# Weight loads of the four FFNs in a trunk kernel: half of a pair's raw blocks in another pool, five chunks instead of four, two sums in place, X's differences by column

## Chip, cores and metric

The kernel runs on one core of a Trainium2 chip. The metric is the device time of one execution in microseconds (us). Before the change the median of three runs is 2451.7 us (2450.68 to 2454.08).

## What is computed

A trunk of DEPTH = 2 layers over 512 tokens of width 1024, all in float32. Each layer is a half-step FFN, a mixer (a bidirectional state-space scan in layer 0, neighbourhood attention in layer 1), a second half-step FFN, and a gated per-layer input embedding ("ple"). The change concerns the four FFNs; cut to that, the reference is:

```python
def swiglu(x, w_gu, w_down):
    g, u = jnp.split(x @ w_gu, 2, axis=-1)
    return (jax.nn.silu(g) * u) @ w_down

for i in range(DEPTH):
    h = h + 0.5 * swiglu(rmsnorm(h, ffn1_norm[i]), ffn1_w_gu[i], ffn1_w_down[i])
    h = h + mixer(rmsnorm(h, mix_norm[i]))
    h = h + 0.5 * swiglu(rmsnorm(h, ffn2_norm[i]), ffn2_w_gu[i], ffn2_w_down[i])
    gate = jax.nn.sigmoid(rmsnorm(h, ple_norm[i]) @ ple_w_gate[i])
    h = h + gate * rmsnorm(p[i] @ ple_w_proj[i], ple_post_norm[i])
```

The width between is 2816, or 22 columns of 128.

## The kernel before

**Products in three matmuls.** A float32 weight tile ("unit") is split into a hi part `wh` (a cast by ScalarE, L195) and a lo part `wl` (raw minus hi, by VectorE, called DVE, L197). The data are split in the same way, and each product is three matmuls: hi x hi, hi x lo, lo x hi. TensorE (PE) runs them; GpSimd (POOL) helps with a few products; SyncE (SP) issues the loads.

**The order of one FFN** (`ffn_order`, L49 to 66). First come six plain columns: for each, gate and up products against the normed data (L246, L249, L250), `activate` (L391 to 400), which makes the column's intermediate. The other 16 columns are made in pairs by a Strassen-like scheme of seven blocks, i = 0 to 6 (`block`, L446). A block is one unit of 128x1024 and 24 matmuls of 128x256 (L455 to 457). Between the blocks stand the "downs" of the chunk before: a down is one of the eight output tiles d, and it multiplies all intermediates of a chunk of columns by a unit of the down weights, three matmuls of 128x512 for each column; its result goes to h (L515). A chunk of six columns (three pairs, 21 blocks) thus carries eight downs of 18 matmuls between its blocks. After the last block stands `between` (in the second FFN of a layer, the ple's projection), then the eight downs of the last chunk, with which the next stage's norm begins.

**What the blocks work on.** The weights' side: for a pair the raws a11, a12, a21, a22 (1024 wide) and the sums s1 = a21 + a22 (L216), s2 = s1 - a11 (L217), s3 = a11 - a21 (L218), s5 = a12 - s2 (L223). Blocks 0 to 6 use a11, s2, s3, s1, a12, s5, a22. X's side: `sums(kk)` (L407 to 442) makes the differences of the normed data, for kk = 0 to 3, during the plain columns 2, 3 and 4, the last two together in column 4; each takes some twelve DVE operations (from L412 to L440). The norm's factor R is there from column 1 on, in the first FFN of all from column 2 on.

**After a block.** Its bank is added up by DVE (L461). At i = 5 and 6 a half of the pair's intermediate is finished: the add, for i = 5 a SiLU on ScalarE (L483), a product on GpSimd (L491), a cast on ScalarE (L496) and the lo part on DVE (L497). A down needs both parts of its columns.

**The loader** (L143 to 236). `plan` lists all units in the order in which TensorE uses them. `unit` keeps three split units ready. Raw tiles stand in `wr`, four buffers of 128x1024, `wh` and `wl` in three each. A plain or down unit ("u") brings on the next load and is split. At a pair's first block ("g") all four raws must be in `wr`, then s1, s2 and s3 are made in tiles of the shared pool `md` (24 buffers, also used for the intermediates and X's parts). Each block's split ("o") starts another load if fewer than three raws wait. A load is a DMA on SyncE's queue; it waits for the last reader of its buffer, and so do those behind it. The code fixes what is done; a scheduler decides where each engine's instructions stand.

Of the kernel before, what the change touches and what calls it, by code (L numbers as in the profile page):

```python
# [21 lines left out]
CHUNKS = ((0, 6), (6, 12), (12, 18), (18, 22))  # L22
# [47 lines left out]
def trunk(ctx, tc, A, out):  # L70
# [110 lines left out]
    loads = iter([src for what, a in todo if what != "o" for src in (a if what == "g" else [a])])  # L181
    todo = iter(todo)
    raws, ready, splits, blocks = [], [], [], {}

    def load_unit():
        src = next(loads, None)
        if src is not None:
            raw = wp.tile([P, 1024], F32, name=nm("wr"), tag="wr", bufs=4)
            n = src.shape[-1]
            sy.dma_start(out=raw[:, :n], in_=src)  # L190
            raws.append((raw, n))
# [11 lines left out]
    def prep_next():  # L203
        item = next(todo, None)
        if item is None:
            return False
        what, a = item
        if what == "u":
            load_unit()
            split_raw(*raws.pop(0))  # L210
        elif what == "g":
            while len(raws) < 4:
                load_unit()
            a21, a22, a11, a12 = [raws.pop(0)[0] for _ in range(4)]
            s1, s2, s3 = wide(), wide(), wide()
            v.tensor_add(out=s1, in0=a21, in1=a22)  # L216
# [1 line left out]
            v.tensor_sub(out=s3, in0=a11, in1=a21)  # L218
            blocks.update({0: a11, 1: s2, 2: s3, 3: s1, 4: a12, 6: a22})
        else:  # L220
            if a == 3:
                blocks[5] = wide()
                v.tensor_sub(out=blocks[5], in0=blocks[4], in1=s_of[0])  # L223
            if a == 1:
                s_of[0] = blocks[1]
            split_raw(blocks.pop(a), 1024)
            if len(raws) < 3:
                load_unit()
        return True

    s_of = [None]
# [122 lines left out]
    def ffn(norm, nxt, between=lambda: None, first=None):  # L354
# [144 lines left out]
        made = None  # L499
# [697 lines left out]
    begun = [(next(loads), wp.tile([P, 1024], F32, name=nm("wr"), tag="wr", bufs=4)) +  # L1197
# [168 lines left out]
```

## Time and profile before

| | before |
|---|---|
| median of 3 runs | 2451.7 us (2450.68 to 2454.08) |
| profiled execution | 2451.2 us, of which the span is 2449.2 us and 2.0 us lie outside it |
| mean granted clock of TensorE | 0.985 |
| busy: PE, DVE, ACT, POOL | 2367.2, 1771.3, 1105.3, 476.3 us |
| DMA | 265.93 MB, 109 GB/s in the mean |
| the four FFNs' first blocks start at | 74.20, 1006.21, 1446.15, 2071.31 us |
| their last eight downs start at | 360.22, 1293.74, 1732.07, 2359.06 us |

A row of the timeline gives the start in us, the duration in us, engine, line, operation, output and inputs, and in brackets the idle time of the engine just before it and what ended that. A matmul's duration overlaps the next one's; what counts is the distance of the starts. A row of the windows gives a stretch, its length, the busy time of each engine in it, the TensorE clock that was granted (1.00 is full), and the DMA engines' share. A row of waits gives the engine, the tile and line that waited, what it waited for, the total, the number and the longest.

### The profile page before, as it was taken

To read this page: it belongs to the slowest core of one execution; us is meant where nothing else is said; L and a number is where in the kernel's file an instruction comes from. 1 tells how busy PE (TensorE), PEld (TensorE's weight loads), DVE (VectorE), ACT (ScalarE), POOL (GpSimd) and SP (SyncE) were. 2 spreads that over 40 slices of the span, in tenths; PEclk is the share of its full clock that TensorE was granted. 3 is DMA by queue.
4 is the path that set the end of the run, shared out by engine and by line. 5 is a ranking of instruction groups with operands and counts; after the bars stand their busy time and mean duration, and the time that the engine had idled before them with its cause. 6 is when DMAs were issued, how large, how long until landed. Compare 5 with 4: busy or idle time off the path is not lost.

```text
span 2449.2 us, 34985 instructions
## 1 busy us (share of the span) xinstructions
PE 2367.2 (97%) x13810; PEld 2049.9 (84%) x13810; DVE 1771.3 (72%) x2437; ACT 1105.3 (45%) x1787; POOL 476.3 (19%) x373
## 2 busy tenths in 40 slices
PE   9999999999999999999999999999999999999898
PEld 8898888888888888898887889888877887899787
DVE  7877658877777767877656787775678758777657
ACT  5433335655566743433335443332437644333243
POOL 0110011345455621011103111110100011011120
PEclk9999999999999999999999999999999999999999
DMA  4233224544444542233223223232442322333222
GB/s 166 84 102 108 78 82 137 175 136 142 140 137 134 171 147 87 88 94 101 89 86 104 91 75 100 95 102 78 145 131 108 113 87 81 102 94 97 85 84 86
DMA packets 94341, 265.93 MB, mean 109 GB/s; under 512 B 11473, under 2 KB 12369, under 8 KB 94177
## 3 DMA queue, kind: packets, MB, share of 16 engines
q1 hardware_dynamic: 93888, 263.57, 34.0%
q8 instruction: 108, 1.77, 0.3%
q14 instruction: 57, 0.46, 0.1%
q10 hardware_dynamic: 288, 0.14, 0.0%
HBM read 253.40 MB, written 10.26 MB: 108 GB/s over the span
## 4 chain that ended last, share of the span: by engine, by line
PE 76%; DVE 12%; ACT 4%; POOL 4%; issue 2%; DMA 1%; SPq 0%; ACTq 0%; POOLq 0%; DVEq 0%
PE ps L250 17%; PE ps L246 17%; PE ps L249 16%; PE ps L455 7%; PE ps L457 7%; PE ps L456 7%; POOL t L491 2%; DVE wl L197 2%; ACT wh L195 2%; DVE md L218 2%; DVE md L216 1%; PE ps L833 1%; DVE md L217 1%; PE ps L811 1%; PE ps L854 1%
## 5 line engine op out<-in xcount | busy, mean ns | idle before, releaser
L246 PE MATMUL ps<-md,wh 128*128 128x512 f32 x2128 | 848.5, 399 | 36.2 <-ACT wh L195 31.9
L250 PE MATMUL ps<-md,wl 128*128 128x512 f32 x2128 | 838.9, 394 | 5.8 <-DVE wl L197 5.8
L249 PE MATMUL ps<-md,wh 128*128 128x512 f32 x2128 | 838.9, 394 | 0.2
L195 ACT CAST wh<-wr 128x1024 fp32r<-128x1024 f32 (+2 forms) x401 | 385.4, 963 | 648.1 <-PE ps L249 313.1
L197 DVE TENSOR_TENSOR wl<-wr,wh 128x1024 fp32r<-128x1024 f32 (+2 forms) x401 | 466.7, 1164 | 153.5 <-ACT wh L195 127.2
L246 PEld LDWEIGHTS ps<-md,wh 128*128 128x128 f32 x2128 | 405.3, 191 | 121.7 <-ACT wh L195 35.0
L250 PEld LDWEIGHTS ps<-md,wl 128*128 128x128 f32 x2128 | 405.2, 190 | 94.2 <-DVE wl L197 9.0
L249 PEld LDWEIGHTS ps<-md,wh 128*128 128x128 f32 x2128 | 406.5, 191 | 82.6 <-issue 3.3
L491 POOL TENSOR_TENSOR t<-t,t 128x512 f32<-128x512 f32 x64 | 121.7, 1902 | 978.4 <-ACT t L483 866.9
L457 PE MATMUL ps<-md,wl 128*128 128x256 f32 x1024 | 291.7, 285 | 4.4 <-DVE wl L197 4.4
L456 PE MATMUL ps<-md,wh 128*128 128x256 f32 x1024 | 291.1, 284 | 0.0
L455 PE MATMUL ps<-md,wh 128*128 128x256 f32 x1024 | 290.8, 284 | 0.0
L455 PE MATMUL ps<-sc,wh 128*128 128x256 f32 x768 | 222.6, 290 | 14.3 <-ACT wh L195 14.3
L457 PE MATMUL ps<-sc,wl 128*128 128x256 f32 x768 | 221.2, 288 | 12.6 <-DVE wl L197 12.6
L461 DVE TENSOR_TENSOR t<-ps,t 128x512 f32<-128x512 f32 x224 | 151.4, 688 | 108.3 <-PE ps L457 107.4
L456 PE MATMUL ps<-sc,wh 128*128 128x256 f32 x768 | 219.3, 286 | 0.0
L457 PEld LDWEIGHTS ps<-md,wl 128*128 128x128 f32 x1024 | 197.8, 193 | 5.2 <-DVE wl L197 5.2
L455 PEld LDWEIGHTS ps<-md,wh 128*128 128x128 f32 x1024 | 197.7, 193 | 1.9
L456 PEld LDWEIGHTS ps<-md,wh 128*128 128x128 f32 x1024 | 197.7, 193 | 1.9
L292 POOL TENSOR_TENSOR sq<-sq,sq 128x512 f32<-128x512 f32 x71 | 100.5, 1415 | 423.9 <-ACT sq L288 421.8
L195 ACT CAST wh<-md 128x1024 fp32r<-128x1024 f32 x128 | 131.7, 1047 | 109.1 <-PE ps L456 68.6
L515 DVE SCALAR_TENSOR_TENSOR hs<-ps,hs 128x512 f32<-128x512 f32 x128 | 88.1, 688 | 126.2 <-PE ps L250 126.2
(205 smaller groups left out, 2989.9 us busy)
## 6 DMA issues: line engine op xcount, KB each, us to landing
wr<-in_w_gw_dram SPq DMA_DIRECT2D x128, 512.0 KB, 3.4
wr<-in_w_dn_dram SPq DMA_DIRECT2D x96, 384.0 KB, 3.3
wr<-in_w_in_dram SPq DMA_DIRECT2D x65, 512.0 KB, 3.8
wr<-in_w_gu_dram SPq DMA_DIRECT2D x44, 512.0 KB, 3.4
hs<-crow SPq DMA_DIRECT2D x64, 256.0 KB, 4.0
wr<-in_w_qkv_dram SPq DMA_DIRECT2D x24, 512.0 KB, 3.5
wr<-in_w_dn_dram SPq DMA_DIRECT2D x32, 256.0 KB, 2.7
hs<-vrow SPq DMA_DIRECT2D x64, 128.0 KB, 3.5
```

Source lines behind the costliest of these rows:

```text
L195: splits.append(s.copy(out=hi[:, :n], in_=raw[:, :n]))
L197: v.tensor_sub(out=lo[:, :n], in0=raw[:, :n], in1=hi[:, :n])
L246: m = te.matmul(out=pt, lhsT=hi[:, sl], rhs=part(xp, 0, cols), start=first and k == 0, stop=False)
L249: te.matmul(out=pt, lhsT=hi[:, sl], rhs=part(xp, 1, cols), start=False, stop=False)
L250: te.matmul(out=pt, lhsT=lo[:, sl], rhs=part(xp, 0, cols), start=False, stop=last and k == n - 1)
L292: (v if fast else g).tensor_add(out=self.acc, in0=self.acc, in1=q)
L455: te.matmul(out=o, lhsT=hi[:, sl], rhs=xh, start=j == 0 and kk == 0, stop=False)
L456: te.matmul(out=o, lhsT=hi[:, sl], rhs=xl, start=False, stop=False)
L457: te.matmul(out=o, lhsT=lo[:, sl], rhs=xh, start=False, stop=j == 1 and kk == 3)
L461: v.tensor_add(out=k[to], in0=pt, in1=k[other])
L491: g.tensor_mul(out=x, in0=x, in1=gate)
L515: v.scalar_tensor_tensor(out=h[d], in0=pt, scalar=0.5, in1=h[d], op0=ALU.mult, op1=ALU.add)
```

## The change

It has four parts, all in the FFNs.

- **Raw blocks.** The pair's loads come in the order a21, a11, a22, a12. The first two go into `wr`, the other two into tiles of `md`. Loads run ahead by two counts, up to three waiting in `wr` and two in `md` (`top_up`, after each step of the plan), instead of one load per step.
- **Chunks** of 6, 4, 4, 4, 4 columns instead of 6, 6, 6, 4. The chunks of pairs are four of two pairs (14 blocks). An FFN has 40 downs instead of 32: 8 of 18 matmuls and 32 of 12, instead of 24 and 8. The number of matmuls is the same.
- **Two sums in place.** s3 is written over a21, and s5 over s2, right behind the split of block 1 instead of ahead of block 3.
- **X's differences by column.** One kk for each plain column from the first that has R: columns 1 to 4, and in the first FFN columns 2, 3, and then two in column 4 as before. The first pair of X11's parts lies in `sc` slots instead of `md`.

```diff
-CHUNKS = ((0, 6), (6, 12), (12, 18), (18, 22))
+CHUNKS = ((0, 6), (6, 10), (10, 14), (14, 18), (18, 22))
...
-                            yield "g", [gw[p - PLAIN // 2, x, y] for x, y in ((1, 0), (1, 1), (0, 0), (0, 1))]
+                            yield "g", [gw[p - PLAIN // 2, x, y] for x, y in ((1, 0), (0, 0), (1, 1), (0, 1))]
...
-    loads = iter([src for what, a in todo if what != "o" for src in (a if what == "g" else [a])])
+
+    loads = [x for what, a in todo if what != "o"
+             for x in (zip(a, ("wr", "wr", "md", "md")) if what == "g" else [(a, "wr")])]
...
+        src, tag = loads.pop(0)
+        raw = wp.tile([P, 1024], F32, name=nm("wr"), tag="wr", bufs=4) if tag == "wr" else wide()
...
+    def top_up():
+        while loads and waiting[loads[0][1]] < {"wr": 3, "md": 2}[loads[0][1]]:
+            load_unit()
...
-            while len(raws) < 4:
-                load_unit()
-            a21, a22, a11, a12 = [raws.pop(0)[0] for _ in range(4)]
-            s1, s2, s3 = wide(), wide(), wide()
+            a21, a11, a22, a12 = [take()[0] for _ in range(4)]
+            s1, s2 = wide(), wide()
             v.tensor_add(out=s1, in0=a21, in1=a22)
             v.tensor_sub(out=s2, in0=s1, in1=a11)
-            v.tensor_sub(out=s3, in0=a11, in1=a21)
-            blocks.update({0: a11, 1: s2, 2: s3, 3: s1, 4: a12, 6: a22})
+            v.tensor_sub(out=a21, in0=a11, in1=a21)
+            blocks.update({0: a11, 1: s2, 2: a21, 3: s1, 4: a12, 5: s2, 6: a22})
         else:
-            if a == 3:
-                blocks[5] = wide()
-                v.tensor_sub(out=blocks[5], in0=blocks[4], in1=s_of[0])
-            if a == 1:
-                s_of[0] = blocks[1]
-            split_raw(blocks.pop(a), 1024)
-            if len(raws) < 3:
-                load_unit()
+            split_raw(blocks[a], 1024)
+            if a == 1:
+                v.tensor_sub(out=blocks[5], in0=blocks[4], in1=blocks[5])
+        top_up()
...
-                if a[0] >= 2:
-                    for kk in ((0,), (1,), (2, 3), ())[a[0] - 2]:
-                        sums(kk)
+                while left and R[0] is not None:
+                    sums(left.pop(0))
+                    if a[0] < 4:
+                        break
```

In these rows of the order, names ending in a number are tiles: `wr` and `md` raws, `in_w_gw1_dram` the pairs' weights and `in_w_dn1_dram` the down weights of the first FFN. First SyncE's loads in the middle of the first FFN, before:

```order
L190 DMA wr282_1648<-in_w_dn1_dram 128x768
L190 DMA wr284_1679<-in_w_dn1_dram 128x768
L190 DMA wr291_1716<-in_w_gw1_dram 128x1024
L190 DMA wr298_1771<-in_w_gw1_dram 128x1024
L190 DMA wr313_1891<-in_w_gw1_dram 128x1024
L190 DMA wr319_1929<-in_w_gw1_dram 128x1024
L190 DMA wr325_1941<-in_w_dn1_dram 128x768
L190 DMA wr329_1976<-in_w_dn1_dram 128x768
```

and of the changed kernel:

```order
L192 DMA md269_1576<-in_w_gw1_dram 128x1024
L192 DMA md270_1578<-in_w_gw1_dram 128x1024
L192 DMA wr239_1377<-in_w_dn1_dram 128x512
L192 DMA wr245_1416<-in_w_dn1_dram 128x512
L192 DMA wr256_1492<-in_w_gw1_dram 128x1024
L192 DMA wr268_1574<-in_w_gw1_dram 128x1024
L192 DMA wr281_1661<-in_w_dn1_dram 128x512
L192 DMA wr287_1700<-in_w_dn1_dram 128x512
```

The two raws of `md` now stand ahead of down loads whose tiles were asked for earlier (the numbers 1377 and 1416 are lower than 1576), and only two pair loads in a row take `wr` buffers.

Next DVE at the change from one pair of columns to the next in the first FFN (in before inside its last chunk, after inside its second chunk). L497 (now L508) is the lo part of a half of the intermediate, L216 to L218 (now L227 to L229) are s1, s2, s3, L461 (now L472) is the add of block 6. Before:

```order
L497 TENSOR_TENSOR md_2536<-t_2444,md_2535 128x2x256
L216 TENSOR_TENSOR md_2543<-wr_2328,wr_2383 128x1024
L515 SCALAR_TENSOR_TENSOR hs_85<-ps_2540,hs_85 128x512
L217 TENSOR_TENSOR md_2544<-md_2543,wr_2472 128x1024
L218 TENSOR_TENSOR md_2545<-wr_2472,wr_2328 128x1024
L461 TENSOR_TENSOR t_2413<-ps_2574,t_2413 128x512
L223 TENSOR_TENSOR md_2702<-wr_2541,md_2544 128x1024
L497 TENSOR_TENSOR md_2536<-t_2413,md_2535 128x2x256
L197 TENSOR_TENSOR wl_2579<-wr_2553,wh_2577 128x768
```

and of the changed kernel:

```order
L508 TENSOR_TENSOR md_1690<-t_1604,md_1689 128x2x256
L227 TENSOR_TENSOR md_1695<-wr_1492,md_1576 128x1024
L472 TENSOR_TENSOR t_1549<-ps_1694,t_1549 128x512
L228 TENSOR_TENSOR md_1696<-md_1695,wr_1574 128x1024
L229 TENSOR_TENSOR wr_1492<-wr_1574,wr_1492 128x1024
L508 TENSOR_TENSOR md_1690<-t_1549,md_1689 128x2x256
L211 TENSOR_TENSOR wl_1739<-wr_1661,wh_1737 128x512
L527 SCALAR_TENSOR_TENSOR hs_81<-ps_1736,hs_81 128x512
L211 TENSOR_TENSOR wl_1759<-md_1696,wh_1757 128x1024
```

The down's split (`wl_2579` before, `wl_1739` now) stands behind the second half in both; s5 (L223) and an eviction (L515) have left the stretch ahead of it, and the add of block 6 now comes ahead of s2.

Last DVE where the plain columns end, in the second FFN. L412 is the first step of a kk of X's differences, L436 to L440 (now L447 to L451) its last ones, L393 and L396 (now L398 and L401) open the activation of column 5, L265 (now L270) is its lo part. Before:

```order
L436 TENSOR_TENSOR t_9205<-t_9193,t_9205 128x256
L412 SCALAR_TENSOR_TENSOR t_9215<-hs_8573,cst,rt_8881 128x512
L437 TENSOR_TENSOR t_9206<-t_9193,t_9205 128x256
L440 TENSOR_TENSOR sc_9202<-t_9205,sc_9201 128x512
L412 SCALAR_TENSOR_TENSOR t_9217<-hs_8749,cst,rt_8881 128x512
L440 TENSOR_TENSOR sc_9204<-t_9206,sc_9203 128x512
L419 TENSOR_TENSOR md_9195<-t_9215,md_9195 128x256
L265 TENSOR_TENSOR md_9221<-t_9217,md_9221 128x512
```

and of the changed kernel:

```order
L447 TENSOR_TENSOR t_9280<-t_9271,t_9280 128x256
L211 TENSOR_TENSOR wl_9303<-wr_9200,wh_9301 128x1024
L448 TENSOR_TENSOR t_9281<-t_9271,t_9280 128x256
L451 TENSOR_TENSOR md_9278<-t_9280,md_9278 128x512
L227 TENSOR_TENSOR md_9292<-wr_9135,md_9202 128x1024
L451 TENSOR_TENSOR md_9279<-t_9281,md_9279 128x512
L228 TENSOR_TENSOR md_9293<-md_9292,wr_9200 128x1024
L229 TENSOR_TENSOR wr_9135<-wr_9200,wr_9135 128x1024
```

Before, the last two kk follow each other in one plain column; now the last kk has that column alone, and the sums of the first pair (L227 to L229) follow it.

More of the change, by code (lines that the diff above doesn't have):

```diff
@@ L180, in trunk, with take @@
     todo = list(plan())
-    loads = iter([src for what, a in todo if what != "o" for src in (a if what == "g" else [a])])
+    loads = [x for what, a in todo if what != "o"
+             for x in (zip(a, ("wr", "wr", "md", "md")) if what == "g" else [(a, "wr")])]
     todo = iter(todo)
     raws, ready, splits, blocks = [], [], [], {}
+    waiting = {"wr": 0, "md": 0}
     def load_unit():
[L186 to L191, printed above, removed]
+        src, tag = loads.pop(0)
+        raw = wp.tile([P, 1024], F32, name=nm("wr"), tag="wr", bufs=4) if tag == "wr" else wide()
+        n = src.shape[-1]
+        sy.dma_start(out=raw[:, :n], in_=src)
+        raws.append((raw, n, tag))
+        waiting[tag] += 1
+    def take():
+        if not raws:
+            load_unit()
+        raw, n, tag = raws.pop(0)
+        waiting[tag] -= 1
+        return raw, n
+    def top_up():
+        while loads and waiting[loads[0][1]] < {"wr": 3, "md": 2}[loads[0][1]]:
+            load_unit()
     def split_raw(raw, n):
@@ L208, in prep_next @@
         if what == "u":
[L209 to L210 removed]
+            split_raw(*take())
         elif what == "g":
[L212 to L215 removed]
+            a21, a11, a22, a12 = [take()[0] for _ in range(4)]
+            s1, s2 = wide(), wide()
             v.tensor_add(out=s1, in0=a21, in1=a22)
             v.tensor_sub(out=s2, in0=s1, in1=a11)
[L218 to L223 removed]
+            v.tensor_sub(out=a21, in0=a11, in1=a21)
+            blocks.update({0: a11, 1: s2, 2: a21, 3: s1, 4: a12, 5: s2, 6: a22})
+        else:
+            split_raw(blocks[a], 1024)
             if a == 1:
[L225 to L228 removed]
+                v.tensor_sub(out=blocks[5], in0=blocks[4], in1=blocks[5])
+        top_up()
         return True
[L231 removed]
     def unit():
@@ L405, in ffn, with sc_r @@
         x11 = []
+        def sc_r():
+            return bp.tile([P, T], F32R, name=nm("sc"), tag="sc", bufs=15)
         def sums(kk):
@@ L413, in sums @@
                                        op1=ALU.mult)
-            if kk % 2 == 0:
-                x11.append(md(F32R))
+            if kk == 0:
+                x11[:] = [sc_r(), sc_r()]
+            elif kk == 2:
+                m = md(F32R)
+                x11[:] = m[:, 0, :], m[:, 1, :]
             c = slice(HT * (kk % 2), HT * (kk % 2) + HT)
-            hl = x11[-1][:, 0, c], x11[-1][:, 1, c]
+            hl = x11[0][:, c], x11[1][:, c]
             s.copy(out=hl[0], in_=x[0][:, lo_])
@@ L427, in room @@
                 if kk < 3:
-                    return [bp.tile([P, T], F32R, name=nm("sc"), tag="sc", bufs=15) for _ in range(2)]
+                    return sc_r(), sc_r()
                 m = md(F32R)
@@ L497, in halve @@
             v.tensor_sub(out=hl[1][:, :, c], in0=x, in1=hl[0][:, :, c])
-        made = None
+        made, left = None, [0, 1, 2, 3]
         for what, *a in ffn_order():
@@ L1195, in trunk @@
     n = Norm(C_G1)
-    begun = [(next(loads), wp.tile([P, 1024], F32, name=nm("wr"), tag="wr", bufs=4)) +
+    begun = [(loads.pop(0)[0], wp.tile([P, 1024], F32, name=nm("wr"), tag="wr", bufs=4)) +
              tuple(md(F32R).rearrange("p a b -> p (a b)") for _ in range(2)) for _ in range(4)]
@@ L1222, in trunk @@
             bring(*o)
-    for _ in range(3):
-        load_unit()
+    top_up()
     sy.dma_start(out=cst[:, C_GM:], in_=A["cst"][:, C_GM:])
```

## Prediction

> **What bounds the kernel now.** I read the page first, then TensorE's waits, then windows over the four FFNs, then single places on the timeline. TensorE works almost all of the time:
>
> ```profile
> span 2449.2 us, 34985 instructions
> PE 2367.2 (97%) x13810; PEld 2049.9 (84%) x13810; DVE 1771.3 (72%) x2437; ACT 1105.3 (45%) x1787; POOL 476.3 (19%) x373
> ```
>
> The change leaves the list of matmuls as it is, so only TensorE's stops can go, and what a stop does to its clock. Its waits (line, tile waited for, total us, times, longest) are nearly all for a weight unit's hi part (`wh`) or lo part (`wl`):
>
> ```profile
> PE ps L246 <- ACT wh L195: 31.9, 8, 4.4
> PE ps L457 <- DVE wl L197: 17.0, 20, 2.2
> PE ps L455 <- ACT wh L195: 14.3, 19, 2.1
> ...
> PE ps L246 <- ACT md L264: 3.8, 2, 1.9
> ```
>
> To see where they lie I cut each FFN in two. The start runs from the first block to the end of the fourth block and first down unit; the middle from there to the first of the last eight downs. The rows are starts, then middles, in the order of the FFNs (length; busy time of PE, PEld, DVE, ACT, POOL; granted clock; DMA share; GB/s):
>
> ```profile
> 74.20:98.16 23.96, 19.53 (x116) 17.96 (x115) 18.94 (x24) 8.62 (x11) 2.13 (x1) 0.86 0.23 72
> 1006.21:1028.70 22.49, 18.12 (x115) 16.44 (x114) 17.49 (x20) 8.61 (x11) 2.13 (x1) 0.92 0.26 77
> 1446.15:1469.23 23.08, 19.14 (x115) 17.50 (x114) 17.50 (x20) 8.71 (x11) 2.14 (x1) 0.85 0.24 74
> 2071.31:2093.83 22.52, 18.15 (x116) 16.51 (x115) 17.49 (x20) 8.62 (x11) 2.13 (x1) 0.92 0.24 76
> 98.16:360.22 262.06, 250.56 (x1665) 230.34 (x1664) 179.97 (x194) 93.27 (x114) 29.95 (x16) 0.98 0.30 92
> 1028.70:1293.74 265.04, 251.28 (x1665) 230.52 (x1663) 181.65 (x195) 94.99 (x116) 30.91 (x16) 0.98 0.31 95
> 1469.23:1732.07 262.84, 251.09 (x1664) 230.69 (x1663) 180.07 (x194) 93.28 (x114) 29.95 (x16) 0.98 0.30 91
> 2093.83:2359.06 265.23, 250.82 (x1665) 230.16 (x1663) 181.79 (x195) 94.98 (x116) 30.92 (x16) 0.98 0.31 95
> ```
>
> What they would last without stops comes from a stretch that has none; the rows are the first matmul of a block, of the next block, of a down unit, and of the block after it:
>
> ```profile
> 105.14 0.28 PE L455 MATMUL ps<-md,wh 128*128 128x256 f32 x1
> ...
> 108.02 0.28 PE L455 MATMUL ps<-sc,wh 128*128 128x256 f32 x1
> ...
> 110.89 0.40 PE L246 MATMUL ps<-md,wh 128*128 128x512 f32 x1
> ...
> 115.00 0.28 PE L455 MATMUL ps<-md,wh 128*128 128x256 f32 x1
> ```
>
> A block takes 108.02 - 105.14 = 2.88 us, a down of 18 matmuls 4.11 (0.228 each; one of 12 then 2.74). A start is 4 x 2.88 + 4.11 = 15.63, a middle 52 x 2.88 + 23 x 4.11 = 244.29. The starts sum to 92.05, 29.5 above nominal; the middles to 1055.17, 78.0 above. Two of the middles end in a wait of 1.9 for the ple's input (the L264 row), so the blocks' part is 78.0 - 3.8 = 74.2. These 29.5 and 74.2 are what the change can work on, and it can add to them.
>
> **The late loads go.** Before, DVE frees a raw buffer at the sums s1 to s3, and the next down's load waits for that. SyncE's queue, ScalarE and TensorE in one such place:
>
> ```profile
> 319.89 5.37 SPq L190 DMA_DIRECT2D wr<-in_w_dn_dram  x3
> ```
>
> ```profile
> 323.08 0.83 ACT L195 CAST wh<-wr 128x768 fp32r<-128x768 f32 x1 [2.64 <-DMA wr<-in_w_dn_dram]
> ```
>
> ```profile
> 323.97 0.80 PE L246 MATMUL ps<-md,wh 128*128 128x512 f32 x1 [4.15 <-ACT wh L195]
> ```
>
> ```profile
> 322.35:325.76 3.41, 1.79 (x5) 1.25 (x6) 1.81 (x2) 2.68 (x3) 0.00 (x0) 0.50 0.30 119
> 325.76:329.17 3.41, 3.41 (x10) 2.64 (x9) 1.50 (x2) 0.05 (x1) 0.00 (x0) 0.50 0.40 115
> ```
>
> It costs 4.15 us of idle and two windows at half clock, of which 0.9 and 1.7 us of work are lost: 6.75. After, the `md` pool takes half of a pair's raws and the SyncE order has every down's load a pair earlier, released by splits long done. A pair lasts 7 x 2.88 + 3 x 2.74 = 28.4 us, so I count no wait for a transfer. A raw for `md` that waited for its buffer would hold SyncE's queue, the next two downs' loads behind it; its buffer was last read a pair back, so I take 0, and 6.75 (rival E) as the other end.
>
> **The pair boundary, 28 times.** In chunks of two pairs each boundary runs block 5, block 6, down, block 0 of the next pair, down, block 1. Let T be the end of block 5, 108.02 in the stretch above, where DVE's and GpSimd's order was the one that it will be:
>
> ```profile
> 112.30 0.69 DVE L497 TENSOR_TENSOR md<-t,md 128x512 fp32r<-128x512 f32 x1 [1.83 <-ACT md L496]
> 112.91 1.22 DVE L216 TENSOR_TENSOR md<-wr,wr 128x1024 f32<-128x1024 f32 x1
> ...
> 115.78 2.32 DVE L218 TENSOR_TENSOR md<-wr,wr 128x1024 f32<-128x1024 f32 x1
> 118.02 0.68 DVE L497 TENSOR_TENSOR md<-t,md 128x512 fp32r<-128x512 f32 x1
> 118.65 1.23 DVE L197 TENSOR_TENSOR wl<-md,wh 128x1024 fp32r<-128x1024 f32 x1
> ```
>
> ```profile
> 109.89 1.73 POOL L491 TENSOR_TENSOR t<-t,t 128x512 f32<-128x512 f32 x1 [23.60 <-ACT t L483]
> 114.81 2.21 POOL L491 TENSOR_TENSOR t<-t,t 128x512 f32<-128x512 f32 x1 [3.19 <-DVE t L461]
> ```
>
> The product of block 5 (GpSimd) and its halves come first, then s1, the add, s2, then s3, which lasts 2.32 because GpSimd's second product runs beside it, then the second half, and only then the next split: T + 10.63. In the changed order that split is the `wl` of the down behind block 0. It is 512 wide; its price:
>
> ```profile
> L197 DVE TENSOR_TENSOR wl<-wr,wh 128x512 fp32r<-128x512 f32 x32 | 24.7, 773 | 20.1 <-ACT wh L195 20.1
> ```
>
> So it is there at T + 10.63 + 0.7 = T + 11.3. TensorE asks for it with that down's third matmul, at T + 2.88 + 2.74 + 2.88 + 2 x 0.228 = T + 8.96: a stop of 2.4. That holds for 5 boundaries in each FFN, 20 in all. Inside chunk 1 the downs still have 18 matmuls and 768 columns (between 0.77 and the 1.23 of 1024, say 1.0): asked for at 10.33, there at 11.6, 1.25 us, 4 times; from chunk 1 to 2 it is 11.3 against 10.33, 1.0 us, 4 times. Together 20 x 2.4 + 9.0 = 57 us.
>
> Each stop can also lower the clock. Neighbouring windows of the FFN2 start:
>
> ```profile
> 1008.42:1011.83 3.41, 1.81 (x16) 1.61 (x14) 3.41 (x4) 0.61 (x1) 0.00 (x0) 1.00 0.00 0
> 1011.83:1015.25 3.42, 1.72 (x12) 1.52 (x13) 3.42 (x5) 1.54 (x3) 0.53 (x1) 1.00 0.52 163
> 1015.25:1018.66 3.41, 3.41 (x16) 3.17 (x16) 1.58 (x3) 2.60 (x4) 1.60 (x1) 0.50 0.17 67
> ```
>
> TensorE busy for 1.72 of a window, and the next is granted 0.50; busy for 1.81, and the next is full. A half window costs 1.7 us of work. A stop of 2.4 leaves about 2.2 idle (the matmuls ahead drain meanwhile). The idle time needed is 3.41 - 1.72 = 1.69, and a window of 3.41 holds that much of 2.2 in (3.41 - 2.2) + 2 x (2.2 - 1.69) = 2.23 of 3.41 positions, 65%. So 13 of the 20 stops bring a half window: 22 us. The short ones bring none. The boundaries sum to 57 + 22 = 79 against 74.2: **+4.8**.
>
> The Trainium skill, "TensorE: Matmul & The Clock Gate", section "What's actually happening", puts the half clock behind an idle window of about 3.4 us; by it no stop of 2.4 would be followed by one, and the boundaries would be 57. The rows above disagree with it, since 1.72 busy of 3.42 was enough.
>
> **The sums of X by column.** In the last three FFNs one column of them per plain column fits under the matmuls, as it does before for the first ones (column's first and last entry on DVE; a plain column lasts 10.9, as the two L396 ends ahead of them show):
>
> ```profile
> 984.65 0.69 DVE L396 TENSOR_TENSOR t<-ps,rt 128x512 f32<-128x512 f32 x1 [0.65 <-PE ps L250]
> ...
> 994.20 0.68 DVE L393 TENSOR_TENSOR t<-ps,rt 128x512 f32<-128x512 f32 x1
> 995.53 0.69 DVE L396 TENSOR_TENSOR t<-ps,rt 128x512 f32<-128x512 f32 x1 [0.64 <-PE ps L250]
> ```
>
> The load is 994.20 - 984.65 = 9.6 of 995.53 - 984.65 = 10.9 us, so DVE arrives at the first block without arrears. What is late next is the down's last pair of matmuls, for the intermediate of column 5, whose split stands behind s5, a 1024-wide pass like the 1.22 of s1: about 1 us, an estimate from that row. In the first FFN two columns of X still fall together, and only its late load goes; ScalarE waited for that:
>
> ```profile
> 85.06 0.83 ACT L195 CAST wh<-wr 128x768 fp32r<-128x768 f32 x1 [1.58 <-DMA wr<-in_w_dn_dram]
> ```
>
> From 8.3 I take 6.2 for it (1.58 and the 0.6 or so that its queue behind it lost). Starts: 3 x 1.0 + 6.2 = 9.2, **-20.3**; if nothing of the first FFN's goes, -18.2, and if DVE stays 2 us behind in the others, -12.
>
> **The ends.** The last down before the final eight is 1.37 us shorter. The two ple inputs come no sooner: 2 x 1.37. In the other two FFNs the last half must be there for the eighth matmul of the first last-down:
>
> ```profile
> 360.63 0.69 DVE L497 TENSOR_TENSOR md<-t,md 128x512 fp32r<-128x512 f32 x1 [1.83 <-ACT md L496]
> ```
>
> That down began at 360.22, so T was 360.22 - 4.11 - 2.88 = 353.23 and the half ends at T + 8.1; now it is wanted at T + 2.88 + 2.74 + 7 x 0.228 = T + 7.2: 0.9 each. **+4.5**.
>
> **What costs nothing by itself.** The change adds 8 downs per FFN: 32 evictions at 0.69 (as other 128x512 rows here), 32 more `wl` splits at 0.77 or less, 32 casts. These 47 us on DVE fall on a DVE busy 72% and lie under the matmuls; if that cover were gone, all 47 would show. In-place s3 and s5 change no duration. Their price is a wait: s3 overwrites a raw that s1 has read, on the same engine, so nothing queues behind it; s5 moves from block 3's place to behind block 1's split, 1.2 us in either place.
>
> **The sum.** 4.8 - 20.3 + 4.5 = -11.0 on the profiled execution's 2451.2 (span 2449.2 and 2.0 outside it): 2440.2. The median, 2451.7, is 0.5 higher; I say 2440. A measurement of this kernel can tell 0.2%, 4.9 us, from no change.
>
> **Rivals.**
> A, no half clock after the 2.4 us stops: boundaries 57, so -17.2 - 15.8 = -33, 2418. For it: the window with 1.81 busy, 1.6 idle, stayed full, and a stop cut by a window's edge stays below that. Against it: 1.72 busy was enough, and 2.2 idle rarely falls so. 10%. The rule of the Trainium skill's page named above would give this case.
> B, the 2.4 us stop is not there because the scheduler's order of DVE runs ahead (GpSimd's first product ends earlier, so the halves do): only the 9.0 of the short ones remain, 9 - 74.2 - 15.8 = -81, 2370. Against it stands the chain above. 7%.
> C, no change: all 20 stops bring a half window, 57 + 34 = 91, +16.8 - 15.8 = +1, 2452. For it: the grid of windows and the pair's 28.4 us could keep in step, and block 5's product, 1.73, could take 2.21 as the second one does, which makes each stop nearly 2.9. 17%.
> D, slower: a boundary stop is followed by two half windows, as the stop at 323.97 was. Then each costs 2.4 + 2.6 = 5.0, 20 x 5.0 + 9 = 109, +34.8 - 15.8 = +19, 2470. The point is (74.2 + 15.8 - 9) / 20 = 4.05 per stop; beyond it the new boundaries cost more than all that went. Against it: a window with 1.81 busy stayed full, and these stops are little over half of 4.15. 9%.
> E, the change does not do what it says: loads still come late, 6.75 at each of the 20, 135 + 9 = 144, +69.8 - 15.8 = +54, 2505. SyncE's order speaks against it. 3%.
>
> **How the numbers follow.** The forecast has 54%; its own range is 2430 to 2449, from 8 to 17 half windows and the first FFN's start. With A and C that is 81%, and the range from A's 2418 to C's 2452, a little beyond each, is 2416 to 2458; B, D and E are left out. Faster by over 0.2% (below about 2447): 53 of the forecast, A, B: 70%. Within it: 1 of the forecast, 15 of C: 16%. Slower: 2 of C, D, E: 14%.
>
> **What would show it.** Right: TensorE's waits for `wh` of a down (31.9 us in 8 times) gone, none over 3 us; some 20 waits for a down's `wl` of about 2.2 instead, about 13 followed by a window at 0.50; starts at 16.6 but for the first FFN's 21.8; waits for the ple's input of 3.3. Wrong: ScalarE's casts of `in_w_dn` still waiting for a DMA (E); no waits for `wl` at block 0's down (B); windows of 1.2 to 1.7 busy followed by full ones (A), or two half ones in a row (D).

## The result, and the profile after

The changed kernel takes 2439.74 us (median of four runs, 2437.59 to 2443.51) against 2452.89 (2450.68 to 2454.08) of the kernel before in the same comparison: a ratio of 0.9949, 95% interval 0.9932 to 0.9966. That is 13.2 us faster. The profiled execution took 2437.86 us, 2436.1 of it the span; against the profiled 2451.2 of before it is 13.3 less. The page of the kernel after:

```profile
span 2436.1 us, 35198 instructions
...
PE 2354.6 (97%) x13810; PEld 2036.8 (84%) x13810; DVE 1799.9 (74%) x2501; ACT 1107.4 (45%) x1819; POOL 481.0 (20%) x373
```

TensorE has the same 13810 matmuls and is busy 12.6 us less, because fewer of them ran at half clock: the trace has 14 windows of 3.41 us at half clock where the trace of before has 22, ahead of the last one at its end. Its waits, after:

```profile
PE ps L255 <- DVE wl L211: 56.7, 32, 2.2
PE ps L251 <- ACT md L269: 8.0, 3, 3.8
PE ps L468 <- DVE wl L211: 2.2, 1, 2.2
```

The waits for a down's `wh` (31.9 us, up to 4.4) are gone, and so are nearly all for the blocks' `wh` and `wl`. In their place stand 32 waits for a `wl` at L255, none longer than 2.2; 28 of them are the changes of pair (one lies in the first FFN's start, three behind FFNs). Two of the three for `md` at L251 are those for the ple's input, 3.77 us each where they were 1.90. The loads themselves show in ScalarE's waits. Before, its casts waited 24 times for a down's load:

```profile
ACT wh L195 <- DMA wr<-in_w_dn_dram: 53.1, 24, 3.6
```

After, there is no such wait at all.

The windows of the kernel after show where the time went. First each FFN from its first block to the end of block 3 of its first pair (four blocks and two downs of 18; nominal, that is without stops, 4 x 2.88 + 2 x 4.11 = 19.74), then each from the first block to the first of the last eight downs (nominal 259.92 in both kernels):

```profile
74.59:101.54 26.95, 22.38 (x133) 19.34 (x132) 20.63 (x26) 8.74 (x11) 3.23 (x1) 0.94 0.35 108
1005.39:1026.01 20.62, 20.09 (x134) 18.17 (x133) 15.37 (x17) 7.51 (x9) 2.03 (x1) 1.00 0.46 142
1439.77:1460.37 20.60, 20.08 (x133) 18.17 (x132) 15.36 (x17) 7.51 (x9) 2.02 (x1) 1.00 0.44 142
2061.31:2081.92 20.61, 20.08 (x134) 18.18 (x132) 15.36 (x17) 7.50 (x9) 2.02 (x1) 1.00 0.48 142
```

```profile
74.59:358.10 283.51, 266.04 (x1778) 243.99 (x1777) 205.45 (x234) 101.61 (x131) 32.68 (x17) 0.99 0.28 88
1005.39:1286.60 281.21, 264.01 (x1778) 242.59 (x1776) 202.46 (x227) 102.87 (x133) 33.60 (x17) 0.99 0.29 93
1439.77:1720.05 280.28, 266.86 (x1777) 245.28 (x1776) 200.26 (x225) 100.38 (x129) 31.56 (x17) 0.98 0.29 89
2061.31:2345.65 284.34, 267.15 (x1778) 245.04 (x1776) 202.51 (x227) 102.84 (x133) 33.59 (x17) 0.98 0.30 92
```

The starts are 88.78 - 4 x 19.74 = 9.8 above nominal. The whole stretches sum to 1129.34, 89.7 above nominal; without the starts and without the two waits for the ple's input (7.5) the changes of pair are 72.3. Before, by the prediction's cut: starts 29.5, changes of pair 74.2, ple waits 3.8. That cut ends the starts one down earlier; the second down of before lasts 4.10 to 4.11 us in all four FFNs, its nominal 4.11, so the two cuts can be compared. The rest of the span grew from 2449.2 - 1147.2 = 1302.0 to 2436.1 - 1129.3 = 1306.8; that is where the last eight downs stand.

One change of pair after, from the second chunk of pairs to the third. VectorE, GpSimd, ScalarE, TensorE:

```profile
220.77 0.69 DVE L508 TENSOR_TENSOR md<-t,md 128x512 fp32r<-128x512 f32 x1 [1.84 <-ACT md L507]
221.38 1.22 DVE L227 TENSOR_TENSOR md<-wr,md 128x1024 f32<-128x1024 f32 x1
222.51 0.69 DVE L472 TENSOR_TENSOR t<-ps,t 128x512 f32<-128x512 f32 x1
223.12 1.22 DVE L228 TENSOR_TENSOR md<-md,wr 128x1024 f32<-128x1024 f32 x1
224.25 2.32 DVE L229 TENSOR_TENSOR wr<-wr,wr 128x1024 f32<-128x1024 f32 x1
226.49 0.68 DVE L508 TENSOR_TENSOR md<-t,md 128x512 fp32r<-128x512 f32 x1
227.09 0.68 DVE L211 TENSOR_TENSOR wl<-wr,wh 128x512 fp32r<-128x512 f32 x1
```

```profile
223.28 2.20 POOL L502 TENSOR_TENSOR t<-t,t 128x512 f32<-128x512 f32 x1 [3.19 <-DVE t L472]
```

```profile
220.64 0.62 ACT L209 CAST wh<-wr 128x512 fp32r<-128x512 f32 x1
```

```profile
225.23 0.40 PE L254 MATMUL ps<-md,wh 128*128 128x512 f32 x1
227.82 0.50 PE L255 MATMUL ps<-md,wl 128*128 128x512 f32 x1 [2.19 <-DVE wl L211]
```

Half, s1, add, s2, s3 stretched to 2.32 beside GpSimd's product, second half, split: the chain that the prediction took from another place of the kernel before. ScalarE had cast the hi part of that unit at 220.64, so neither its load nor its cast held the split up. TensorE's next matmul should have started 0.228 after 225.23 and started at 227.82: the stop costs 2.36 and, with the slower matmul behind it, 2.47. It stands so 20 times.

### The profile page after: what moved, and what is told of

It is laid out like the page before. It is cut to its first block, busy times and chain, and to the rows that moved or that the text cites. A ratio compares the mean times of both kernels' runs of the same rounds, so it can differ in the third digit from the quotient of the medians.

```text
span 2436.1 us, 35198 instructions
## 1 busy us (share of the span) xinstructions
PE 2354.6 (97%) x13810; PEld 2036.8 (84%) x13810; DVE 1799.9 (74%) x2501; ACT 1107.4 (45%) x1819; POOL 481.0 (20%) x373
## 3 DMA queue, kind: packets, MB, share of 16 engines
q8 instruction: 108, 1.77, 0.3%
## 5 line engine op out<-in xcount | busy, mean ns | idle before, releaser
L255 PE MATMUL ps<-md,wl 128*128 128x512 f32 x2128 | 841.7, 396 | 56.7 <-DVE wl L211 56.7
L251 PE MATMUL ps<-md,wh 128*128 128x512 f32 x2128 | 846.7, 399 | 8.5 <-ACT md L269 8.0
L255 PEld LDWEIGHTS ps<-md,wl 128*128 128x128 f32 x2128 | 404.4, 190 | 155.4 <-DVE wl L211 70.6
L211 DVE TENSOR_TENSOR wl<-wr,wh 128x1024 fp32r<-128x1024 f32 (+2 forms) x401 | 427.9, 1067 | 116.4 <-ACT wh L209 90.9
L251 PEld LDWEIGHTS ps<-md,wh 128*128 128x128 f32 x2128 | 404.9, 190 | 91.8 <-ACT md L269 10.0
L254 PEld LDWEIGHTS ps<-md,wh 128*128 128x128 f32 x2128 | 405.1, 190 | 85.3 <-issue 3.3
L502 POOL TENSOR_TENSOR t<-t,t 128x512 f32<-128x512 f32 x64 | 124.3, 1942 | 974.0 <-ACT t L494 876.3
L209 ACT CAST wh<-md 128x1024 fp32r<-128x1024 f32 x160 | 167.4, 1046 | 275.0 <-PE ps L467 263.3
L472 DVE TENSOR_TENSOR t<-ps,t 128x512 f32<-128x512 f32 x224 | 151.7, 689 | 157.5 <-PE ps L468 157.5
L466 PE MATMUL ps<-sc,wh 128*128 128x256 f32 x896 | 253.8, 283 | 1.6 <-ACT wh L209 1.6
L467 PE MATMUL ps<-sc,wh 128*128 128x256 f32 x896 | 254.0, 284 | 0.0
L468 PE MATMUL ps<-md,wl 128*128 128x256 f32 x896 | 253.6, 283 | 0.0
L467 PE MATMUL ps<-md,wh 128*128 128x256 f32 x896 | 253.5, 283 | 0.0
L466 PE MATMUL ps<-md,wh 128*128 128x256 f32 x896 | 253.4, 283 | 0.0
L211 DVE TENSOR_TENSOR wl<-md,wh 128x1024 fp32r<-128x1024 f32 x160 | 195.2, 1220 | 25.7 <-ACT wh L209 25.7
L466 PEld LDWEIGHTS ps<-sc,wh 128*128 128x128 f32 x896 | 172.4, 192 | 6.0 <-ACT wh L209 2.0
L467 PEld LDWEIGHTS ps<-sc,wh 128*128 128x128 f32 x896 | 172.2, 192 | 3.9
L468 PEld LDWEIGHTS ps<-sc,wl 128*128 128x128 f32 x896 | 172.1, 192 | 2.4 <-DVE wl L211 2.4
```

Of the source, the lines that this page charges most:

```text
L209: splits.append(s.copy(out=hi[:, :n], in_=raw[:, :n]))
L211: v.tensor_sub(out=lo[:, :n], in0=raw[:, :n], in1=hi[:, :n])
L251: m = te.matmul(out=pt, lhsT=hi[:, sl], rhs=part(xp, 0, cols), start=first and k == 0, stop=False)
L254: te.matmul(out=pt, lhsT=hi[:, sl], rhs=part(xp, 1, cols), start=False, stop=False)
L255: te.matmul(out=pt, lhsT=lo[:, sl], rhs=part(xp, 0, cols), start=False, stop=last and k == n - 1)
L466: te.matmul(out=o, lhsT=hi[:, sl], rhs=xh, start=j == 0 and kk == 0, stop=False)
```

## Experiments

All times are medians of four or more timed runs, compared with the kernel before on the same chip.

| kernel | us | ratio to before (95%) |
|---|---|---|
| changed kernel | 2439.7 | 0.9949 (0.9932 to 0.9966) |
| chunks alone | 2592.3 | 1.0572 (1.0555 to 1.059) |
| old chunks, the rest changed | 2384.5 | 0.9726 (0.9711 to 0.974) |
| old place of X's differences | 2452.6 | 1.0004 (0.9994 to 1.0013) |
| sums not in place | 2443.7 | 0.9962 (0.9948 to 0.9976) |
| early sums | 2367.4 | 0.9659 (0.9644 to 0.9673) |
| second product on VectorE | 2391.9 | 0.9754 (0.9739 to 0.9768) |
| downs one block later | 2368.8 | 0.9659 (0.9645 to 0.9674) |
| s1 twice | 2434.0 | 0.9919 (0.9902 to 0.9935) |
| early ple input | 2427.6 | 0.9896 (0.988 to 0.9912) |
| early sums, old chunks | 2353.0 | 0.9593 (0.9579 to 0.9607) |
| the same with early ple input | 2346.7 | 0.9568 (0.9554 to 0.9582) |

The theory: a stop at a change of pair is set by the place of the down's `wl` in VectorE's order, behind s1, s2, s3 and the second half. The rivals: it is the amount of work on VectorE there, GpSimd's products, or still a load.

### Chunks alone

The kernel before with one line changed:

```diff
-CHUNKS = ((0, 6), (6, 12), (12, 18), (18, 22))
+CHUNKS = ((0, 6), (6, 10), (10, 14), (14, 18), (18, 22))
```

> The kernel before with the new chunks (6, 4, 4, 4, 4) alone, loader and sums as before. My theory: at each of the 20 boundaries with a 12-matmul down behind block 0 the load still waits for s3, as in the one such place of before (4.15 us idle and two half windows, 6.75): about 20 x 6.75 + 9 = 144 against 74 in the middle and about 6 at the ends, so 2452 + 70 + 6 = about 2530 us. Rival: the order and not the loads set the boundary, then each costs as in the changed kernel, about 2.5 to 4: 2460.

It took 2592, slower than the 2530 of the theory. Its waits, and one change of pair in it on VectorE, SyncE, ScalarE and TensorE:

```profile
PE ps L246 <- ACT wh L195: 158.8, 32, 6.9
```

```profile
322.21 2.30 DVE L218 TENSOR_TENSOR md<-wr,wr 128x1024 f32<-128x1024 f32 x1
```

```profile
324.54 4.46 SPq L190 DMA_DIRECT2D wr<-in_w_dn_dram  x3
```

```profile
327.30 0.62 ACT L195 CAST wh<-wr 128x512 fp32r<-128x512 f32 x1 [2.74 <-DMA wr<-in_w_dn_dram]
```

```profile
327.97 0.80 PE L246 MATMUL ps<-md,wh 128*128 128x512 f32 x1 [5.03 <-ACT wh L195]
```

s3 ends at 324.51, the down's load is issued at 324.54, and TensorE stands for 5.03 us. SyncE's queue waits for an s3 (L218) 32 times in this kernel, once for each pair. So the late load comes from the raw buffer that s3 frees, as supposed. The theory took the stop from the place with 18 matmuls (4.15); with 12 the down is wanted earlier, and the 8 changes of pair in and behind chunk 1 and the starts are late too (32 waits, 28 at changes of pair and 4 at starts, where it counted 20 long ones). The 2460 of the rival is refuted.

### Old chunks

The changed kernel with that line the other way round.

> The changed kernel with the chunks of before (6, 6, 6, 4), so the loader, the sums in place and X's differences by column without the chunks. My theory: the loader took the late loads away wherever they were, and the regular place of block 0 and a down behind it, 7 times in an FFN, is what the chunks add. In chunks of three pairs the order puts the sums of every third pair ahead of the halves, and the down behind block 0 comes there at only one or two of seven changes of pair: some 6 us per FFN in the middle instead of 18 to 20, and the ends 1 to 2.5 shorter: about 2385 us. Rival: the wider chunks hold more intermediates in the shared pool, raws wait for buffers there, and loads are late again: 2440 or more.

2384.5 against 2385. Together with the one before this gives a square: with the old loader the new chunks cost 2592 - 2452 = 140 us, with the new one 2439.7 - 2384.5 = 55. The new loader, the sums and X's differences are together worth 67 us in the old chunks and 153 in the new; no run has the loader alone. The chunks are a loss in either case. TensorE's waits in this kernel are short and few:

```profile
PE ps L468 <- DVE wl L211: 10.2, 13, 2.2
PE ps L255 <- DVE wl L211: 9.1, 7, 2.1
```

### Old place of X's differences

```diff
-                while left and R[0] is not None:
-                    sums(left.pop(0))
-                    if a[0] < 4:
-                        break
+                if a[0] >= 2:
+                    for kk in ((0,), (1,), (2, 3), ())[a[0] - 2]:
+                        sums(kk)
```

> The changed kernel with X's differences in the columns of before (kk 0, 1, then 2 and 3 together from column 2 on). My theory: the starts of the second to fourth FFN go from 0.9 us above nominal back to about 7, so 3 x 6 = 18 us slower than the changed kernel: about 2458 us, and TensorE waits again for wl and wh of blocks 0 and 1 there. Rival: those starts gained from the loader, and the place of the differences is worth less than 5 us: 2440 to 2445.

12.8 us slower than the changed kernel, not 18. The starts of this kernel, in the cut of above:

```profile
74.53:102.99 28.46, 23.85 (x133) 21.08 (x132) 20.64 (x26) 8.74 (x11) 3.20 (x1) 0.88 0.32 103
1006.59:1032.10 25.51, 22.21 (x134) 19.24 (x132) 19.17 (x22) 8.73 (x11) 3.25 (x1) 0.93 0.35 115
1448.32:1473.80 25.48, 20.82 (x134) 18.22 (x133) 19.17 (x22) 8.72 (x11) 3.20 (x1) 1.00 0.37 116
2073.26:2098.74 25.48, 20.80 (x133) 18.20 (x132) 19.18 (x22) 8.73 (x11) 3.21 (x1) 1.00 0.35 115
```

They are 5.7 to 5.8 above nominal in the last three FFNs against 0.9: 3 x 4.9 = 14.6 come from the place of the differences (and 1.5 in the first FFN, by a half window). The other 1.1 to 1.7 of each (6.9 to 7.5 before, in the cut of the prediction) came with the other three parts; which of them was not separated.

### Sums not in place

s3 and s5 in tiles of their own, otherwise the changed kernel:

```diff
-            v.tensor_sub(out=a21, in0=a11, in1=a21)
+            v.tensor_sub(out=s3, in0=a11, in1=a21)
...
-                v.tensor_sub(out=blocks[5], in0=blocks[4], in1=blocks[5])
+                blocks[5] = wide()
+                v.tensor_sub(out=blocks[5], in0=blocks[4], in1=blocks[1])
```

> The changed kernel with s3 and s5 in tiles of their own. My theory: in place they save buffers and no time; the order at the changes of pair is the same, the raw that s3 no longer overwrites comes free earlier, and nothing waits for a load: within 4 us of the changed kernel, 2437 to 2444 us. Rival: two more tiles of the pool per pair make the raws wait: over 2450 us.

2443.7, inside the expected band and 4.0 above the changed kernel, with overlapping intervals of the ratio: in place is no cost, and its gain, if any, is about what a measurement of this kernel can tell.

### Early sums

The sums leave the chain: a pair's s1, s2 and s3 are written ahead of block 6's split of the pair before.

```diff
-                        if i_ == 0:
-                            yield "g", [gw[p - PLAIN // 2, x, y] for x, y in ((1, 0), (0, 0), (1, 1), (0, 1))]
-                        yield "o", i_
+                        if (p, i_) == (PLAIN // 2, 0):
+                            yield "g", pair(p)
+                        if i_ == 6 and p + 1 < NF // 2:
+                            yield "g", pair(p + 1)
+                        yield "o", (p, i_)
```

> The changed kernel with the next pair's s1, s2 and s3 written in the code ahead of the split of block 6 of the pair before (the first pair of an FFN keeps its place). My theory: the stop at each change of pair (2.19 us idle, 2.47 above nominal, 20 times, and 1.1 to 1.4 the other 8 times) is there because the down's lo part stands on VectorE behind s1, s2, s3 and the second half. Without the sums in that chain the split is wanted later than it is ready: the 28 waits of TensorE for wl go, and the half windows behind them, about 70 us, so about 2370 us. Rival 1: the chain is bound by GpSimd's two products and the halves; then a stop of 1 us or more stays at each of the 20, about 2405. Rival 2: VectorE waits for the raws of the next pair, which are wanted earlier now, and holds everything behind: 2440 or more.

2367.4 against 2370. Of the 32 waits for a `wl` (L264 here) the 28 at the changes of pair are gone, and the four elsewhere are left:

```profile
PE ps L260 <- ACT md L278: 8.0, 3, 3.8
PE ps L264 <- DVE wl L217: 5.1, 4, 2.1
```

VectorE does the same work, only earlier. Its order changes by more than the sums: the down's split now stands ahead of the second half too (216.56 against 219.09 at the change from the second chunk of pairs to the third), and is there long before the third matmul of the down at 220.05. Behind the second half, which ends at 219.78, a split of 0.68 would have been ready at about 220.4, an estimate from these rows: 0.4 late instead of 2.4. So the sums make most of the stop, and the halves and products alone little of it. The second rival's wait exists but is mostly hidden: at 2187.63 s2 waited 2.54 us for a raw of the next pair, and that cost TensorE 0.56 once, inside a pair.

### Second product on VectorE

```diff
-                g.tensor_mul(out=x, in0=x, in1=gate)
+                (g if i == 5 else v).tensor_mul(out=x, in0=x, in1=gate)
```

> The changed kernel with the product of block 6 (the second of a pair) on VectorE instead of GpSimd. My theory: s3 no longer shares its time with a GpSimd product, so it lasts 1.22 us instead of 2.32, and the second half goes behind the down's split; the product itself adds 0.69 ahead of it. The split is then ready at T + 10.3 instead of 11.3 against T + 8.96: the 20 stops shrink from 2.47 us above nominal to about 1.4, none is long enough for a half window (8 of them now), together 20 x 1.07 + 13 = 34 us: about 2405 us. Rival: s3 is slow for another reason (its place, its operands), it stays at 2.3, and the stops grow by 0.7: about 2460.

2391.9, still faster than expected. VectorE and TensorE at a change of pair:

```profile
222.05 1.22 DVE L229 TENSOR_TENSOR wr<-wr,wr 128x1024 f32<-128x1024 f32 x1
223.19 0.69 DVE L502 TENSOR_TENSOR t<-t,t 128x512 f32<-128x512 f32 x1
223.79 0.68 DVE L211 TENSOR_TENSOR wl<-wr,wh 128x512 fp32r<-128x512 f32 x1
```

```profile
224.53 0.50 PE L255 MATMUL ps<-md,wl 128*128 128x512 f32 x1 [1.09 <-DVE wl L211]
```

s3 takes 1.22 instead of 2.32 as soon as no GpSimd product runs beside it. The product (L502, 0.69) stands ahead of the split in the place of the second half (0.68), which went behind it, so the 1.1 of s3 is what the chain loses. The stop is 1.09 idle instead of 2.19 (1.37 above nominal, the 1.4 expected), and no half window stands behind any of them. The 13 us beyond the expectation: the 8 short stops fell to 0.3 or nothing, about 9 us, and the ends are shorter.

### Downs one block later

```diff
-            while d < KD and (d + 0.5) * len(blocks) <= KD * (n + 1):
+            while d < KD and (d + 0.5) * len(blocks) <= KD * n or d < KD and n == len(blocks) - 1:
```

> The changed kernel with each down one block later (block 0, block 1, down, ..., block 5, down, block 6; the last of a chunk behind its last block). In the order VectorE's chain at a change of pair inside a chunk then is first half, s1, s2, s3 without a GpSimd product beside it, the down's split; the add of block 6 and the second half come behind. My theory: the split is ready at T + 9.7 and wanted at T + 8.96, 0.7 us at 4 changes of pair per FFN and none from chunk to chunk, and no half windows; the ends have 2.7 us more for the last half and the ple's input: about 72 - 12 + 8 less, about 2372 us. Rival: what matters is how much VectorE has to do between block 5 and block 1, the stop moves to block 1's wl and stays above 2 us: 2420 or more.

2368.8 against 2372. In the code nothing changes but which block a down stands behind. TensorE's waits for a down's `wl` fall from 56.7 us to

```profile
PE ps L255 <- DVE wl L211: 17.1, 23, 2.1
```

of which 12 are stops of 0.49 and 8 of 0.81 at changes of pair. VectorE's order changes with it: inside a chunk s3 takes 1.22 (at 184.63), the down's split follows at 185.77, and the add of block 6, GpSimd's product and the second half come behind. So this run takes the stop away by a change of order alone, but does not part the place on TensorE from the place on VectorE.

### s1 twice

```diff
             v.tensor_add(out=s1, in0=a21, in1=a22)
+            v.tensor_add(out=s1, in0=a21, in1=a22)
```

> The changed kernel with s1 computed twice, the second time over the first: one more pass of 1.2 us on VectorE at each pair. In the order that follows, the down's split stands ahead of s2 and s3 at the changes of pair, and the second half, an eviction and block 1's split behind them. My theory: it is the place of the split and not the amount of work that makes the stop. The down's split is ready at T + 8.4, before it is wanted (T + 8.96); block 1's split is ready at T + 13.1 against T + 11.5, so a stop of 1.6 above nominal stays there, too short for half windows: 20 x 0.8 + 13 less, about 2411 us, faster although VectorE does more. Rival: VectorE's load between block 5 and block 1 sets the stop; then it grows by 1.1 at 28 places and half windows follow nearly each: 2475 or more.

2434.0, 5.7 less than the changed kernel with 32 passes more (their runs do not overlap, the intervals of their ratios just do): the amount of work does not set the stop (the rival's 2475). But only a fifth of the 29 us that the theory gave it came. VectorE, GpSimd and TensorE at a change from chunk to chunk:

```profile
225.84 1.77 DVE L211 TENSOR_TENSOR wl<-wr,wh 128x512 fp32r<-128x512 f32 x1
...
229.81 0.68 DVE L509 TENSOR_TENSOR md<-t,md 128x512 fp32r<-128x512 f32 x1
```

```profile
224.87 2.20 POOL L503 TENSOR_TENSOR t<-t,t 128x512 f32<-128x512 f32 x1 [3.19 <-DVE t L473]
```

```profile
227.67 0.50 PE L256 MATMUL ps<-md,wl 128*128 128x512 f32 x1 [0.45 <-DVE wl L211]
230.54 0.51 PE L255 MATMUL ps<-md,wh 128*128 128x512 f32 x1 [1.43 <-DVE md L509]
```

Two things were left out of the expectation. GpSimd's product now falls on the split and stretches it from 0.68 to 1.77. And at a change of chunk the down needs the intermediate that the second half completes, which now comes later. The stop of 2.47 became two or three short ones of about the same sum, with 4 half windows at them instead of 8 in the profiled run.

### Early ple input, and the combinations

`ple_proj` is parted: its load and its two splits are called at block 3 of the last pair.

```diff
+                if a == [NF // 2 - 1, 3]:
+                    prs = early()
                 block(*a)
```

> The changed kernel with the ple's input loaded and split in the last pair's block 3 instead of behind the last block. My theory: the waits of 3.77 us ahead of the ple's projection (in the second FFN of each layer, with half windows behind them 5.9 to 6.4 together) are ScalarE's two casts standing behind the last half in its queue; without them TensorE goes on at once, and what stays there is no more than 0.5: 11 to 12 us less, about 2428 us. Rival: the projection's own weights are late behind them, and half of it stays: 2434.

2427.6 against 2428: the two ends cost 12 us with what follows them. By the profiled runs 7.5 of it are the two waits, which are gone, and most of the rest the three half windows beside them. In the changed kernel the casts (L269) stood behind the last half (L507) on ScalarE:

```profile
1284.89 0.62 ACT L507 CAST md<-t 128x512 fp32r<-128x512 f32 x1 [2.66 <-POOL t L502]
1285.41 0.61 ACT L209 CAST wh<-wr 128x512 fp32r<-128x512 f32 x1
1285.93 1.13 ACT L269 CAST md<-md 128x512 fp32r<-128x512 f32 x2
```

```profile
1286.60 1.65 PE L251 MATMUL ps<-md,wh 128*128 128x512 f32 x3 [3.77 <-ACT md L269]
```

Early sums in the old chunks:

> Early sums (as in early_sums) and the chunks of before together. My theory: with the sums out of the chain there is no stop left at any change of pair in either chunking, so only the ends differ: the last down before the final eight is 1.37 us longer, which takes 1.04 off two ends and about 2.4 (with the half windows) off the two others, some 7 us: about 2360 us. Rival: with chunks of six the shared pool holds four more intermediates, the early sums and raws wait for it, and some loads are late: 2370 to 2390.

and with the early ple input as well:

> Early sums, the chunks of before and the early ple input together, with the changed kernel's loader, in-place sums and X's differences. My theory: early sums and old chunks leave 2.2 us at each of the two ends with a ple and 7 us at the first FFN's start; the early input takes the first away: 2353 - 4.4 = about 2349 us. Rival: three more tiles of the pool are held in the last pair and a raw waits: 2353 or more.

2353.0 and 2346.7, where 2360 and 2349 were expected. Why the first is 7 us better than expected was not looked into. The last is the fastest here, 0.9568 of before; TensorE is busy 2326.5 us of its span of 2343.3.

## Why the prediction was right, and where not

The forecast was 2440 and 11.0 us less than before on the profiled execution; 2439.7 and 13.3 less were measured. That it fits so well is partly luck: the changes of pair came out 6.7 us lower than forecast and the ends 4.0 higher, and these two errors cancel in part.

- **The late loads go.** Right: of 24 waits for a down's transfer none is left. Chunks alone shows the cause, the buffer freed by s3, at 5.03 us a time.
- **The pair boundary.** Mechanism, place and size right: 2.4 predicted, 2.36 to 2.47 measured, 20 times; 1.25 and 1.0 predicted for the short ones, 1.4 and 1.1 measured. Early sums remove it by moving the sums from where they meet the down's split; downs one block later shrink it to 0.49 and 0.81; the product on VectorE shortens it by the 1.1 that s3 loses beside GpSimd's product.
- **The half windows.** Here a term was mis-sized: 13 of 20 stops with a half window, 22 us, were forecast; the profiled run has 8, some 13. The step of the prediction that failed is its limit of 1.72 busy, read from a window that held two stops among its few matmuls. Windows of the changed kernel with one stop of 2.19, each with the window behind it, and one of the kernel with the old place of X's differences:

```profile
1551.15:1554.56 3.41, 1.49 (x7) 1.24 (x8) 3.41 (x5) 2.62 (x4) 0.00 (x0) 1.00 0.39 94
1554.56:1557.98 3.42, 3.42 (x14) 3.04 (x13) 3.42 (x5) 0.62 (x1) 0.00 (x0) 0.50 0.49 131
2274.78:2278.19 3.41, 1.66 (x12) 1.23 (x11) 3.41 (x4) 1.87 (x3) 1.51 (x1) 1.00 0.00 0
2278.19:2281.60 3.41, 2.97 (x15) 2.55 (x16) 3.41 (x5) 1.68 (x3) 0.00 (x0) 1.00 0.57 154
```

```profile
1562.78:1566.19 3.41, 1.55 (x12) 1.12 (x10) 3.41 (x4) 1.97 (x3) 1.41 (x1) 1.00 0.00 0
1566.19:1569.61 3.42, 3.08 (x16) 2.64 (x17) 3.42 (x5) 1.65 (x3) 0.00 (x0) 1.00 0.58 153
```

  1.49 busy was followed by 0.50, 1.55 and 1.66 by 1.00. Busy time counts each matmul to its own end, which runs past the next start, and so counts too much at each stop. At their steps of 0.12 and 0.228 us the matmuls of the prediction's window come to 1.37 and those of the one at 1551.15 to 1.38, and those of the two that were followed by a full one to 1.38 and 1.49 (estimates from their starts): one limit of about 1.38 fits all four. For a window with one stop that is about 1.53 busy. With it the prediction's own working gives (3.41 - 2.19) + 2 x (2.19 - 1.88) = 1.84 of 3.41 positions, 11 of 20; that 8 came is a matter of where the stops lay. The boundaries came to 72.3 instead of 79, so -1.9 instead of +4.8. The runs of the changed kernel spread over 5.9 us, as much as three or four half windows of 1.65; that their number differs from run to run was not tried.
- **X's differences and the starts.** -20.3 forecast, -19.7 measured. Three starts are 0.9 above nominal, as forecast (1.0); the first FFN's is 7.2 instead of 6.2, with one half window (at 83.42) still behind its stops. The run with the old place of the differences shows that 16.1 of it (14.6 and 1.5) come from the place of the differences, and 3.6 with the other parts.
- **The ends.** +4.5 forecast, +8.5 measured: 3.7 in the two waits for the ple's input (3.77 each instead of 1.90; 3.3 was forecast), 4.8 in the rest of the span, of which 2.1 are the waits for the last half (1.04 each, 0.9 forecast). The 0.5 that each ple wait is over is a cast on ScalarE: the cast of the next unit came behind the ple's casts before (at 1294.11) and stands ahead of them now (at 1285.41, in the rows of the early ple input), which takes 0.52. Of the 2.7 that remain, 0.8 lie behind the first ple wait, beside which stand two half windows instead of one; the other 1.9 are spread over stretches that the change leaves alone, and were not looked into.
- **What costs nothing.** Right, but the load was counted too high: 47 us. The 32 evictions are there, but more downs of fewer columns have narrower splits; in all, those of the downs are

```profile
L211 DVE TENSOR_TENSOR wl<-wr,wh 128x512 fp32r<-128x512 f32 x128 | 89.9, 702 | 20.3 <-ACT wh L209 20.3
L211 DVE TENSOR_TENSOR wl<-wr,wh 128x768 fp32r<-128x768 f32 x32 | 30.6, 955 | 0.0
```

  and VectorE's busy time rose from 1771.3 to 1799.9, by 28.6. A slip that no term of the sum used: a pair has four downs, not three, so it lasts 7 x 2.88 + 4 x 2.74 = 31.1 us and not 28.4.
- **The rivals.** A (no half clock) falls: 8 of 20 stops of 2.19 us were followed by one. The Trainium skill, "TensorE: Matmul & The Clock Gate", section "What's actually happening", has the half clock follow an idle window of about 3.4 us. Here a window with 1.49 of 3.41 busy was enough, and the measurement decides. The same section has windows of 3413 ns; the half windows here last 3.41. B is near what early sums made on purpose: its price was 2370, the kernel took 2367, with the 8 short stops gone as well. C and D needed more half windows than came, and block 5's product, which C feared at 2.21, took 1.74. E falls with the waits for `wh`. The break-even of 4.05 us per stop was not reached: 20 stops cost (72 - 10) / 20 = 3.1 with their half windows.

## What to carry to other kernels

Where one engine is busy 97% of the time, make the nominal length of each stretch first and read the excess: it says where the stops are and what a change can win or lose there. A gain in some parts (67 us by the loader, the sums and X's differences in the old chunks) can be spent by another part of the same change (55 us by the chunks); a square of four kernels shows it, one run does not. When a stop follows from the order on a second engine, move the work out of the meeting place, on either engine, before making it shorter.

## What the runs showed of the hardware

- A VectorE pass over two SBUF tiles that began during a GpSimd product of two SBUF tiles ended about its own length after that product. s3 (128x1024, 1.22 us alone) began 0.97 us into a product of 2.20, lasted 2.32 and ended 1.09 after it; with s1 twice a 128x512 split (0.68 alone) began 0.97 into the same product, lasted 1.77 and ended 0.54 after it. s2, begun 0.16 ahead of the product, kept its 1.22. So the 1.1 that both lost is no fixed price but the rest of the product: elsewhere in the kernel after, a 128x1024 split that began 0.26 us into a GpSimd product of 0.61 (at 507.86) lasted 1.43.
- Twenty stops of 1.09 us idle brought no half-clock window; of twenty of 2.19 us, 8 did. Whether one does depends on how the stop lies in a grid of windows of 3.41 us: in each trace here all changes of the granted clock lie on one such grid.
- One more pass of 1.2 us on VectorE, 32 times, did not make the kernel slower (2434.0 against 2439.7): the order that it brought about mattered more than the work.
